# Hybrid trunk layer: attention as two head streams, residual on VectorE, gate weights side by side, and a planner that counts the overhead of a float32r product

## The chip, the cores and the metric

The kernel runs on one core of one Trainium2 chip. The metric is the time of one execution in microseconds (us) of device time, from the first to the last instruction with what the launch adds around them; lower is better. Engine names are those of the profile: PE is TensorE (matmuls), PEld its weight loads, DVE VectorE, ACT ScalarE, POOL GpSimd, SP the engine that only issues transfers.

## The reference

One layer of a trunk, for 1024 prompt tokens and 64 sample tokens (1088 columns in the kernel). One input projection feeds three token mixers and the gates; the three results are projected, gated, summed and projected once more.

```python
cols = x @ lw['w_in'] + lw['b_in']                       # 9864 columns
...
ya, ... = rwkv7_branch(a_cols, ...)                      # A: 8 heads x 64, a chain over chunks
yb, ... = mlstm_branch(b_qk, b_v, b_i, b_f, ...)         # B: 4 heads x 128; b_i, b_f have 4 columns each
yc = stick_breaking(heads_c(c_q), kc, vc, k_past, v_past)  # C: 8 heads x 64
ys = jnp.stack([ya * jax.nn.silu(a_z), yb * jax.nn.silu(b_z), yc * jax.nn.silu(c_z)], axis=2)
br = jnp.einsum('btnc,ncd->btnd', ys, lw['w_branch'])
g = jax.nn.sigmoid(gates.reshape(Bn, T, N_BRANCH, D_MODEL))
mix = jnp.sum(g * br, axis=2) @ lw['w_out']
x = layer_norm(DEEPNORM_ALPHA * x + mix, lw['ln_g'], lw['ln_b'])
x = x + (p @ lw['w_ple']) * jax.nn.sigmoid(x @ lw['w_ple_gate'])
```

Stick breaking, per head and block of 128 queries: z = q k / 8; A[t,s] is sigmoid(z_ts) times the product of 1 - sigmoid(z_tj) over s < j < t; the output is A v. The kernel makes the running product by a scan along the keys and A by the difference of neighbours.

## The kernel before, in words

**Products.** Large products are made in float32r. A number x is split into xh (its float32r rounding) and xl (the rest), a weight likewise into h and l, and a product is three matmuls, h·xh, h·xl and l·xh (`three`, L791). The input projection is 78 blocks of up to 128 columns; a block is 8 slices of the contraction times three token groups (`GR`: 384, 384 and 320 columns), so 72 matmuls. Splitting a block's weights is one ACT copy (h) and one DVE subtraction (l) (`wsplit`, L767). The block of the mLSTM gates has M = 36 columns: four input gates at 0 and four forget gates at 32.

**Order.** The kernel writes its own instruction order: it is one Python program that plans a clock for each engine while it emits. The main stream (`main`, L887) emits the blocks of the projection, then the merge of the three branches (`merge`, L1066), then the tail. Side tasks (generators) run beside it: an operation of a side task is emitted when the planned time at which its operands are ready has been reached by the planned clock of PE (`when`, `step`). So what `mm` (L313) counts for a float32r product (1 ns + columns / 2.4, or 213 ns below 256 columns) sets how many products of the main stream stand between two steps of a side task. DVE, ACT and POOL operations of side tasks are emitted when their engine's planned backlog is below 1.2 us. Among side tasks the lower priority number goes first (residual 3, the mixers' sequence 5).

**Sequence of the side tasks.** `side` (L980) runs the RWKV branch (A: fronts, inverses on POOL, chains over 17 chunks for each of four pairs of heads), then mLSTM (B), then attention (C), then `m_prep`, which takes memory and converts the first branch's result for the merge (`yconv(0)`, L1038: loads of `yd` and `yz` by SP, two DVE operations and one ACT copy for each of eight half tiles). The main stream begins the merge only when `m_prep` has set `prepared` (`m_begin`, L1031).

**The beginning.** An order written by hand (`INTRO`) normalises the input, transposes it and makes the first two blocks. Its last act is to spawn `resid` (L733), which scales and shifts the nine tiles of the normalised input in place by two POOL operations of 128x1024 each and stores them for the tail.

**Attention.** For each of four pairs of heads, `sbpair` (L1749) copies q and k of both heads into float32r parts, transposes v and then k (storing both), spawns for each head `sbhead` (scores, sigmoid, scan, difference) and `sbsum` (transposes of A and products with v), runs `sbsample` (the sample's attention over the cache), loads the next pair and waits until both heads' sums are done:

```python
for h in range(2):
    st = [0, 0]
    self.S.spawn(self.sbhead(p, h, R, st), f"C{p}{h}")
    self.S.spawn(self.sbsum(p, h, R, st, left), f"D{p}{h}")
yield from self.sbsample(p, R)
if p < 3:
    yield from self.sbload(p + 1, R)
yield lambda: left[0] == 0
```

The k transposes are kept in the buffer that is also head 1's scan buffer (`c1`); the v transposes in that of the sample.

Of the kernel before, what the change touches and what calls it, by code (L numbers as in the profile page):

```python
# [16 lines left out]
D = 1024  # L17
# [289 lines left out]
class K:  # L307
# [5 lines left out]
    def mm(self, out, lhsT, rhs, start, stop, more=False):  # L313
        n, w = fsize(out), 0.82 * fsize(lhsT)
        if lhsT.dtype == F32R:
            c = d = 1 + (213.0 if n < 256 else n / 2.4)
        else:
            d = 1 + 2 * n / 2.4
            c = d + max(d, w)
# [413 lines left out]
    def resid(self, xts):  # L733
# [8 lines left out]
        for t, x in enumerate(xts):  # L742
            m = 128 if t < 8 else 64
            for j, op in enumerate((OP.mult, OP.add)):
                yield self.tt(x[:m, :1024], x[:m, :1024], r3[:m, j, :], op, "g")
# [21 lines left out]
    def wsplit(self, i, e="v"):  # L767
# [5 lines left out]
        self.act(h[:, :kc, :M], r[:, :kc, :M], AF.Copy)  # L773
        self.tt(l[:, :kc, :M], r[:, :kc, :M], h[:, :kc, :M].bitcast(F32), OP.subtract, e)
# [16 lines left out]
    def three(self, b, i, g, k, hl, mh, ml):  # L791

        (kc, M), (h, l), (t0, n) = self.ws[i][1:], hl, GR[g]
        x1, x2 = mh[:, k, t0:t0 + n], ml[:, k, t0:t0 + n]
        self.mm(b[:M, :n], h[:, k, :M], x1, k == 0, False)
# [206 lines left out]
    def b_gates(self, i):  # L1002
# [719 lines left out]
    def c_all(self):  # L1722
# [26 lines left out]
    def sbpair(self, p, R):  # L1749
        self.S.note(f"   C {p}")  # L1750
        qs, O = R["qs"], self.O
        hp = slice(2 * p, 2 * p + 2)
        q, k, vv = R["q"], R["k"], R["svv"].r[:, :2304].rearrange("p (c h s d) -> p c h s d", h=2, s=2, d=64)
        for i in range(2):
            r, o = slice(64 * i, 64 * i + 64), slice(64 - 64 * i, 128 - 64 * i)
            x, y = R[f"sq{i}"], R[f"sk{i}"]
# [5 lines left out]
            yield self.tt(R[f"sl{i}"].r[r, :NT], k[r, :NT], y[r, :NT], OP.subtract)  # L1762
        for j, nm in ((2, "v"), (1, "k")):
            f, t = R[nm], R[nm + "t"]
            for c0 in (0, 4, 8):
                m = min(4, 9 - c0)
                w = 128 if c0 < 8 else 64
                b = yield from self.bank()
                for i in range(m):
                    o = (c0 + i) * 128  # L1770
                    yield self.tr(b[:w, i * 128:(i + 1) * 128], f[:, o:o + w])
                s = slice(c0 * 128, (c0 + m) * 128)
                yield self.act(t[:w, s], b[:w, :m * 128], AF.Copy)
                if nm == "v":
                    hi, lo = (vv[:w, c0:c0 + m, :, i, :] for i in range(2))
                    b4 = b[:w, :m * 128].rearrange("p (c h d) -> p c h d", h=2, d=64)
                    yield self.act(hi, b4, AF.Copy)
                    yield self.tt(lo, b4, hi.bitcast(F32), OP.subtract)
                self.unbank(b)
                yield  # L1780
            op, os = (O["sbk_p"], O["sbk_s"]) if j == 1 else (O["sbv_p"], O["sbv_s"])
            t3 = t.v(9, 128)
            yield self.dma(op[0, 0][:, hp, :].rearrange("(a t) h d -> t a (h d)", t=128), t3[:, 0:8, :], "s")
            yield self.dma(os[0, 0][:, hp, :].rearrange("t h d -> t (h d)"), t3[:64, 8, :], "s")
            if nm == "v":
                yield self.act(R["sv"][:64, :128], t[:64, 1024:1152], AF.Copy)
        left = [2]
        self.S.note(f"     heads {p}")
        for h in range(2):
            st = [0, 0]  # L1790
# [441 lines left out]
```

## Time and profile before

| | |
|---|---|
| time, median of 3 runs | 1767.66 us (1766.98 to 1769.55) |
| the profiled execution | 1766.9 us, of which span 1765.1 us |
| PE busy | 1711.2 us, 97% of the span |
| DVE, ACT, POOL busy | 1154.9 (65%), 792.6 (45%), 493.6 us (28%) |
| matmuls | 10873 |
| moved by DMA | 212.10 MB, mean 120 GB/s |
| mean granted TensorE clock | 0.994 |

How to read it: "busy" is the time in which at least one instruction of the engine runs. Matmuls are pipelined, so a busy PE can still be slower than its best; how many products pass in a stretch tells that. The granted clock is a share of 2.4 GHz: 1.00 is that level, 0.50 the level of 1.2 GHz. The kernel's stages in the span, by their instructions: the order by hand and the beginning of A up to about 200 us, A to about 704, B to about 968, C (attention) to about 1363, the merge to about 1534, then the tail.

### The profile page before, as it was taken

The numbers are of one execution on the slowest core, as the hardware profiler recorded it, in microseconds if no ns is written. First come the engines' busy times: TensorE is split into PE (matmuls) and PEld (weight loads), VectorE is DVE, ScalarE is ACT, GpSimd is POOL, SyncE is SP. The second block draws the span as 40 slices with busy tenths as digits, with TensorE's granted clock in tenths as the row PEclk, the third lists the DMA queues.
The fourth block names the chain that finished last, engine by engine and source line by source line (L and its number), as shares of the span: only waits on it lengthen the run. The fifth ranks groups of instructions, "written<-read, shape, count | busy, mean of one in ns | idle before, by whom it ended". The sixth has DMA issues, their size and how long they took to land.

```text
span 1765.1 us, 30061 instructions
## 1 busy us (share of the span) xinstructions
PE 1711.2 (97%) x10873; PEld 1587.3 (90%) x10873; DVE 1154.9 (65%) x2640; ACT 792.6 (45%) x1823; POOL 493.6 (28%) x969
## 2 busy tenths in 40 slices
PE   6979999999999999999999999999999899999999
PEld 5979987888888999999999999999999899988787
DVE  8476467686777655878643665757475568787743
ACT  6434455554445445454445555464553322322421
POOL 6644567266457341321011202111130000000100
PEclk9989999999999999999999999999999999999999
DMA  5533323323333333444335323343322877631421
GB/s 158 175 112 112 97 69 95 107 70 101 95 88 83 100 93 117 161 141 145 111 121 155 120 74 110 97 122 98 106 80 74 257 233 240 225 119 60 148 81 54
DMA packets 224635, 212.10 MB, mean 120 GB/s; under 512 B 53540, under 2 KB 192598, under 8 KB 224486
## 3 DMA queue, kind: packets, MB, share of 16 engines
q1 hardware_dynamic: 197518, 169.50, 32.3%
q10 hardware_dynamic: 22552, 29.02, 4.6%
q0 software_dynamic: 4416, 11.66, 2.1%
q8 instruction: 86, 1.41, 0.3%
q14 instruction: 63, 0.52, 0.1%
HBM read 136.81 MB, written 73.36 MB: 119 GB/s over the span
## 4 chain that ended last, share of the span: by engine, by line
PE 83%; DVE 9%; ACT 4%; issue 2%; DMA 1%; POOL 0%; ACTq 0%; SPq 0%; DVEq 0%; POOLq 0%
PE bk L321 78%; PE bk L328 5%; DVE heap L376 3%; ACT heap L353 3%; DVE heap L358 2%; DVE heap L371 2%; DVE whl L358 1%; DMA heap<-yz 1%; DMA heap<-in_x_prompt_dram 1%; ACT whl L353 0%; DVE heap L412 0%; DVE xl L358 0%; ACTq L431 0%; DVE heap L381 0%; DVE heap L409 0%
## 5 line engine op out<-in xcount | busy, mean ns | idle before, releaser
L321 PE MATMUL bk<-xh,whl 128*128 128x384 f32 (+3 forms) x3792 | 1057.5, 339 | 0.3 <-DVE heap L376 0.3
L321 PEld LDWEIGHTS bk<-xh,whl 128*128 128x128 f32 (+1 forms) x3792 | 682.1, 188 | 12.3 <-issue 3.4
L321 PE MATMUL bk<-xl,whl 128*128 128x384 f32 (+3 forms) x2184 | 669.6, 328 | 1.2 <-POOL xl L360 0.7
L321 PEld LDWEIGHTS bk<-xl,whl 128*128 128x128 f32 (+1 forms) x2184 | 404.4, 188 | 5.5 <-POOL xl L360 1.4
L353 ACT ACTIVATE heap<-bk 64x64 f32<-64x64 f32 (+9 forms) x679 | 219.5, 335 | 370.6 <-PE bk L321 147.8
L360 POOL TENSOR_TENSOR heap<-heap 32x30 f32<-32x30 f32 (+14 forms) x480 | 267.9, 558 | 36.3
L328 PE MATMUL bk<-ident,heap 128*128 128x128 f32 (+3 forms) x942 | 174.9, 277 | 14.1 <-ACT heap L353 12.1
L358 DVE TENSOR_TENSOR whl<-heap,whl 128x1024 fp32r<-128x1024 f32 (+1 forms) x114 | 122.8, 1079 | 91.0 <-ACT whl L353 84.8
L358 DVE TENSOR_TENSOR heap<-heap 128x256 f32<-128x256 f32 (+16 forms) x352 | 168.0, 483 | 11.8 <-DMA heap<-yz 3.4
L321 PE MATMUL bk<-heap 128*128 128x128 f32 (+7 forms) x886 | 157.6, 293 | 8.7 <-ACT heap L353 7.8
L353 ACT ACTIVATE heap<-bk,pc 128x384 f32<-128x384 f32 (+5 forms) x218 | 114.1, 548 | 104.5 <-PE bk L321 79.8
L328 PEld LDWEIGHTS bk<-ident,heap 128*128 128x128 f32 (+3 forms) x942 | 119.7, 142 | 29.6 <-issue 14.9
L321 PEld LDWEIGHTS bk<-heap 128*128 128x128 f32 (+3 forms) x886 | 117.8, 182 | 30.7 <-ACT heap L353 19.9
L353 ACT ACTIVATE whl<-heap 128x1024 fp32r<-128x1024 f32 (+1 forms) x116 | 105.3, 911 | 72.8 <-PE bk L321 54.7
L353 ACT ACTIVATE heap<-heap 64x64 f32<-64x64 f32 (+10 forms) x330 | 113.1, 347 | 45.4 <-DVE heap L376 18.4
L321 PE MATMUL bk<-heap,heap 32*32 32x32 f32 (+3 forms) x1058 | 125.7, 244 | 6.9 <-ACT heap L353 6.4
L321 PEld LDWEIGHTS bk<-heap,heap 128*128 128x128 f32 (+2 forms) x1058 | 98.7, 152 | 31.7 <-ACT heap L353 17.6
L401 DVE TENSOR_TENSOR_SCAN heap<-heap,cst 128x512 f32<-128x512 f32 (+8 forms) x68 | 96.2, 1417 | 45.6 <-POOL heap L418 26.1
L321 PE MATMUL bk<-heapr,whl 128*128 128x384 f32 (+2 forms) x648 | 118.0, 341 | 4.6 <-ACT heapr L353 4.0
L321 PE MATMUL bk<-heapr 128*128 128x256 f32 (+2 forms) x524 | 119.4, 329 | 0.0
L321 PEld LDWEIGHTS bk<-heapr,whl 128*128 128x128 f32 x648 | 110.0, 191 | 10.4 <-ACT heapr L353 5.1
L353 ACT ACTIVATE heap<-bk,hb 128x384 f32<-128x384 f32 (+1 forms) x120 | 67.6, 563 | 113.0 <-PE bk L321 94.7
(154 smaller groups left out, 1819.6 us busy)
## 6 DMA issues: line engine op xcount, KB each, us to landing
heap<-in_w_in_dram SPq DMA_DIRECT2D x77, 512.0 KB
heap<-gt SPq DMA_DIRECT2D x24, 544.0 KB
gt<-heap ACTq DMA_DIRECT2D x48, 192.0 KB
heap<-crd SPq DMA_DIRECT2D x12, 544.0 KB
heap<-yd SPq DMA_DIRECT2D x24, 272.0 KB
heap<-yz SPq DMA_DIRECT2D x24, 272.0 KB
heap<-in_w_branch_dram SPq DMA_DIRECT2D x24, 256.0 KB
xsd<-heap SPq DMA_DIRECT2D x24, 192.0 KB
```

The lines of the kernel that those rows point to most:

```text
L321: lambda: self.nc.tensor.matmul(out, lhsT, rhs, start=start, stop=stop, skip_group_check=more),
L328: lambda: self.nc.tensor.transpose(out, in_, self.ident[:p, :p]), load=(0.82 * fsize(in_), d))
L353: return self.nc.scalar.activation(out, in_, func, **kw)
L358: lambda: self.nc.vector.tensor_tensor(out=out, in0=a, in1=b, op=op))
L360: lambda: self.nc.gpsimd.tensor_tensor(out=out, in0=a, in1=b, op=op))
L371: lambda: q.tensor_scalar(out=out, in0=a, scalar1=s1, scalar2=s2, op0=op0, **kw))
L376: lambda: self.nc.vector.scalar_tensor_tensor(out=out, in0=a, scalar=s, in1=b, op0=op0, op1=op1))
L401: return self.S.emit("dve", fsize(out) * 2.13 + 90, rd, [out], lambda: self.nc.vector.tensor_tensor_scan(out=out, data0=d0, data1=d1, init ...
```

## The change

Four edits. (1) The planner counts 13 ns instead of 1 ns over the columns of a float32r product. (2) The residual's two operations per tile go from POOL (128x1024) to DVE (two halves of 128x512 each). (3) The gate block's l is written into columns 64 to 99 of h, so that one matmul of 100 columns makes h·x and l·x; two matmuls (for xh and xl) take the place of three, and DVE adds the two halves of the result before the store, which the ACT queue issues. (4) Attention is three kinds of tasks: one sequence that loads a pair, transposes k and v and runs the sample, and one stream for each head, which goes to the next pair's copies and scores when its own sums of the last pair are done. Head 1 also waits for the k transposes; the values' transposes wait for both heads' sums of the last pair; the sums wait for the values.

```diff
     def mm(self, out, lhsT, rhs, start, stop, more=False):
         n, w = fsize(out), 0.82 * fsize(lhsT)
         if lhsT.dtype == F32R:
-            c = d = 1 + (213.0 if n < 256 else n / 2.4)
+            c = d = 13 + (213.0 if n < 256 else n / 2.4)
...
             for j, op in enumerate((OP.mult, OP.add)):
-                yield self.tt(x[:m, :1024], x[:m, :1024], r3[:m, j, :], op, "g")
+                for o in (0, 512):
+                    yield self.tt(x[:m, o:o + 512], x[:m, o:o + 512], r3[:m, j, o:o + 512], op)
             yield self.dma(self.resd[t, :m], x[:m, :1024], "s")
...
         self.act(h[:, :kc, :M], r[:, :kc, :M], AF.Copy)
+        if M < 64:
+            l = h[:, :, 64:]
         self.tt(l[:, :kc, :M], r[:, :kc, :M], h[:, :kc, :M].bitcast(F32), OP.subtract, e)
...
+        if M < 64:
+
+            for j, x in enumerate((x1, x2)):
+                self.mm(b[:64 + M, :n], h[:, k, :64 + M], x, k + j == 0, k == kc - 1 and j == 1)
+            return
         self.mm(b[:M, :n], h[:, k, :M], x1, k == 0, False)
         self.mm(b[:M, :n], h[:, k, :M], x2, False, False)
         self.mm(b[:M, :n], l[:, k, :M], x1, False, k == kc - 1)
...
                 self.act(d[r, :n], bank[r, :n], AF.Identity, bias=self.gb[r, 0:1])
+                self.tt(d[r, :n], bank[64 + 32 * j:68 + 32 * j, :n], d[r, :n], OP.add)
                 self.dma(gd[j, :, t0:t0 + n], d[r, :n], "a")
...
-        yield from self.sbload(0, B)
+        self.cld = self.ckt = self.cvt = 0
+        self.cpr, self.csm = [0, 0], [0, 0]
+        for h in range(2):
+            self.S.spawn(self.sbheads(h, B), f"C{h}")
         for p in range(4):
             yield from self.sbpair(p, B)
+        yield lambda: min(self.csm) == 4
...
     def sbpair(self, p, R):
...
+        yield from self.sbload(p, R)
+        self.cld = p + 1
+        yield lambda: min(self.cpr) > p
+        yield from self.sbturn(p, R, 1, "k")
+        self.ckt = p + 1
+        yield lambda: min(self.csm) >= p
+        yield from self.sbturn(p, R, 2, "v")
+        self.cvt = p + 1
+        self.S.note(f"     values {p}")
+        yield from self.sbsample(p, R)
+
+    def sbheads(self, h, R):
+
+        r, o = slice(64 * h, 64 * h + 64), slice(64 - 64 * h, 128 - 64 * h)
+        q, k, x, y, qs = R["q"], R["k"], R[f"sq{h}"], R[f"sk{h}"], R["qs"]
+        for p in range(4):
+            yield lambda: self.cld > p
             yield self.act(x.r[r, :NT], q[r, :NT], AF.Copy)
             yield self.tt(x.r[o, :NT], q[r, :NT], x[r, :NT], OP.subtract)
...
+            self.cpr[h] = p + 1
+            yield lambda: self.csm[h] >= p and (h == 0 or self.ckt > p)
+            self.S.note(f"     head {p}{h}")
+            st = [0, 0]
+            self.S.spawn(self.sbsum(p, h, R, st), f"D{p}{h}")
+            yield from self.sbhead(p, h, R, st)
...
+    def sbturn(self, p, R, j, nm):
...
-        yield lambda: left[0] == 0
...
-    def sbsum(self, p, h, R, st, left):
+    def sbsum(self, p, h, R, st):
...
+        yield lambda: self.cvt > p
         for G in range(4):
...
-        left[0] -= 1
+        self.csm[h] = p + 1
```

`sbturn` holds the transposes, copies and stores that stood in `sbpair`, for one of k and v; the order of the two is turned round.

## Rows read from the trace of the kernel before

**Rows 1.** The page, part 1: busy time, share of the span and number of instructions of each engine.

```profile
PE 1711.2 (97%) x10873; PEld 1587.3 (90%) x10873; DVE 1154.9 (65%) x2640; ACT 792.6 (45%) x1823; POOL 493.6 (28%) x969
```

**Rows 2.** Busy time by stretch, two stretches of the merge; columns: stretch in us from the span's start, its length, busy us of each engine with the number of its instructions in brackets, granted clock of PE, share of the DMA engines, GB/s.

```profile
1408.00:1452.00 44.00, 44.00 (x268) 44.00 (x267) 29.36 (x52) 9.78 (x16) 0.00 (x0) 1.00 0.73 232
1452.00:1496.00 44.00, 44.00 (x270) 44.00 (x269) 36.52 (x69) 10.21 (x18) 1.16 (x2) 1.00 0.76 246
```

**Rows 3.** Groups of PE instructions, each shape apart, whole run: the products of the gate block. Columns: line, engine, operation, names, contraction*weight columns, partitions x columns, count, busy us, mean ns of one.

```profile
L321 PE MATMUL bk<-xh,whl 128*36 128x384 f32 x32 | 8.8, 341 | 0.0
...
L321 PE MATMUL bk<-xl,whl 128*36 128x384 f32 x16 | 5.4, 336 | 0.0
...
L321 PE MATMUL bk<-xh,whl 128*36 128x320 f32 x16 | 4.8, 339 | 0.0
...
L321 PE MATMUL bk<-xl,whl 128*36 128x320 f32 x8 | 2.5, 308 | 0.0
```

**Rows 4.** What PE waited for, stretch 60 to 112 us. Columns: us in total, times, longest us.

```profile
PE bk L321 <- DVE heap L376: 11.8, 1, 11.8
```

**Rows 5.** POOL in order of time, 60 to 105 us: start, us, line, operation, count; L360 with 128x1024 is the residual.

```profile
60.09 4.93 POOL L360 TENSOR_TENSOR heap<-heap,heap 128x1024 f32<-128x1024 f32 x2 [6.31 <-ACT heap L353]
...
78.43 13.41 POOL L360 TENSOR_TENSOR heap<-heap,heap 128x1024 f32<-128x1024 f32 x5
...
92.11 12.60 POOL L360 TENSOR_TENSOR heap<-heap,heap 128x1024 f32<-128x1024 f32 x5
```

**Rows 6.** Groups of DVE instructions, shapes apart, 84.87 to 109 us (columns as in rows 3; idle time before them at the end).

```profile
L358 DVE TENSOR_TENSOR heap<-heap 128x256 f32<-128x256 f32 x4 | 5.8, 1474 | 0.0
L371 DVE TENSOR_SCALAR heap<-heap,der 128x256 f32<-128x256 f32 x2 | 4.7, 2342 | 0.0
L401 DVE TENSOR_TENSOR_SCAN heap<-cmask,heap 128x256 f32<-128x256 f32 x1 | 2.8, 2773 | 0.0
...
L376 DVE SCALAR_TENSOR_TENSOR heap<-bk,der,heap 128x384 f32<-128x384 f32 x2 | 1.2, 606 | 0.0
```

**Rows 7.** The same view, 116 to 135 us, where POOL runs nothing but copies of one column.

```profile
L358 DVE TENSOR_TENSOR heap<-heap 128x256 f32<-128x256 f32 x4 | 1.6, 418 | 0.0
L376 DVE SCALAR_TENSOR_TENSOR heap<-bk,der,heap 128x384 f32<-128x384 f32 x2 | 1.2, 618 | 3.0 <-ACT heap L353 1.7 <-issue 1.3
...
L371 DVE TENSOR_SCALAR heap<-heap,der 128x256 f32<-128x256 f32 x2 | 0.7, 367 | 0.0
...
L401 DVE TENSOR_TENSOR_SCAN heap<-cmask,heap 128x256 f32<-128x256 f32 x1 | 0.7, 692 | 0.0
```

**Rows 8.** Busy time by stretch around that wait (columns as in rows 2).

```profile
60.00:84.87 24.87, 24.87 (x152) 24.29 (x151) 8.41 (x13) 9.16 (x20) 24.47 (x14) 1.00 0.62 206
...
97.47:109.46 11.99, 0.17 (x1) 0.00 (x0) 11.95 (x11) 0.00 (x0) 10.89 (x6) 0.67 0.20 78
...
109.46:115.16 5.70, 5.70 (x20) 5.52 (x20) 2.01 (x6) 1.20 (x4) 0.00 (x0) 0.50 0.19 66
```

**Rows 9.** DVE groups of the whole run: the nearest forms to the new operations.

```profile
L358 DVE TENSOR_TENSOR heap<-heap 128x512 f32<-128x512 f32 x23 | 15.8, 688 | 0.5
...
L358 DVE TENSOR_TENSOR heap<-bk,heap 64x256 f32<-64x256 f32 x32 | 13.2, 413 | 23.1 <-ACT heap L353 22.9
```

**Rows 10.** The chain that ended last, 1362 to 1400 us: start, us, what.

```profile
1374.07 3.71 DMA heap<-yz
...
1386.37 3.21 DMA heap<-yz
...
1391.97 8.09 PE bk L321 x39
```

**Rows 11.** Busy time by stretch: the first products of the merge (columns as in rows 2).

```profile
1380.87:1395.00 14.13, 9.53 (x35) 7.00 (x34) 6.88 (x10) 3.67 (x6) 0.00 (x0) 0.76 0.82 264
```

**Rows 12.** The queue of SP in order of time: the first load of the conversion for the merge.

```profile
1363.64 0.53 SPq L431 DMA_DIRECT2D heap<-yd  x1
```

**Rows 13.** DVE in order of time, from the last scan of one pair of heads to the first of the next.

```profile
1035.57 2.30 DVE L401 TENSOR_TENSOR_SCAN heap<-heap,cst 128x1024 f32<-128x1024 f32 x1 [1.48 <-POOL heap L423]
...
1054.54 0.42 DVE L358 TENSOR_TENSOR heap<-bk,heap 64x256 f32<-64x256 f32 x1 [2.33 <-ACT heap L353]
...
1073.16 0.42 DVE L401 TENSOR_TENSOR_SCAN heap<-heap,cst 128x128 f32<-128x128 f32 x1 [4.75 <-POOL heap L418]
```

**Rows 14.** Busy time by stretch: A, B and C (columns as in rows 2).

```profile
200.00:704.00 504.00, 487.68 (x3508) 438.19 (x3507) 342.22 (x1138) 254.36 (x757) 250.05 (x470) 1.00 0.34 94
704.00:968.00 264.00, 263.46 (x1718) 255.87 (x1717) 169.96 (x451) 127.95 (x296) 53.61 (x128) 1.00 0.44 139
968.00:1364.00 396.00, 395.97 (x2604) 383.17 (x2603) 253.50 (x291) 209.61 (x384) 69.48 (x207) 1.00 0.33 98
```

**Rows 15.** What PE waited for, stretch 200 to 704 us (columns as in rows 4).

```profile
PE bk L321 <- ACT heap L353: 14.2, 27, 1.6
```

**Rows 16.** Groups of PE instructions, the main stream's products of 384 columns (columns as in rows 3): first two 200 to 704 us, last two 968 to 1364 us.

```profile
L321 PE MATMUL bk<-xh,whl 128*128 128x384 f32 x795 | 245.0, 355 | 0.0
L321 PE MATMUL bk<-xl,whl 128*128 128x384 f32 x397 | 133.3, 336 | 0.0
...
L321 PE MATMUL bk<-xh,whl 128*128 128x384 f32 x699 | 206.1, 345 | 0.0
L321 PE MATMUL bk<-xl,whl 128*128 128x384 f32 x349 | 117.2, 336 | 0.0
```

More of the change, by code (lines that the diff above doesn't have):

```diff
@@ L1750, in sbpair @@
         self.S.note(f"   C {p}")
[L1751 to L1756, printed above, removed]
+        yield from self.sbload(p, R)
[13 more added lines that the diff above has]
+            yield lambda: self.cld > p
             yield self.act(x.r[r, :NT], q[r, :NT], AF.Copy)
@@ L1761, in sbpair @@
             yield self.act(y.r[o, :NT], k[r, :NT], AF.Copy)
[L1762 to L1784, printed above, removed]
-            if nm == "v":
-                yield self.act(R["sv"][:64, :128], t[:64, 1024:1152], AF.Copy)
@@ L1787, in sbpair @@
[L1787 to L1790, printed above, removed]
-            self.S.spawn(self.sbhead(p, h, R, st), f"C{p}{h}")
-            self.S.spawn(self.sbsum(p, h, R, st, left), f"D{p}{h}")
-        yield from self.sbsample(p, R)
-        if p < 3:
-            yield from self.sbload(p + 1, R)
-        yield lambda: left[0] == 0
+            yield self.tt(R[f"sl{h}"].r[r, :NT], k[r, :NT], y[r, :NT], OP.subtract)
+            self.cpr[h] = p + 1
@@ new lines, in sbheads @@
+            yield lambda: self.csm[h] >= p and (h == 0 or self.ckt > p)
[4 more added lines that the diff above has]
+    def sbturn(self, p, R, j, nm):
+        O = self.O
+        hp = slice(2 * p, 2 * p + 2)
+        vv = R["svv"].r[:, :2304].rearrange("p (c h s d) -> p c h s d", h=2, s=2, d=64)
+        f, t = R[nm], R[nm + "t"]
+        for c0 in (0, 4, 8):
+            m = min(4, 9 - c0)
+            w = 128 if c0 < 8 else 64
+            b = yield from self.bank()
+            for i in range(m):
+                o = (c0 + i) * 128
+                yield self.tr(b[:w, i * 128:(i + 1) * 128], f[:, o:o + w])
+            s = slice(c0 * 128, (c0 + m) * 128)
+            yield self.act(t[:w, s], b[:w, :m * 128], AF.Copy)
+            if nm == "v":
+                hi, lo = (vv[:w, c0:c0 + m, :, i, :] for i in range(2))
+                b4 = b[:w, :m * 128].rearrange("p (c h d) -> p c h d", h=2, d=64)
+                yield self.act(hi, b4, AF.Copy)
+                yield self.tt(lo, b4, hi.bitcast(F32), OP.subtract)
+            self.unbank(b)
+            yield
+        op, os = (O["sbk_p"], O["sbk_s"]) if j == 1 else (O["sbv_p"], O["sbv_s"])
+        t3 = t.v(9, 128)
+        yield self.dma(op[0, 0][:, hp, :].rearrange("(a t) h d -> t a (h d)", t=128), t3[:, 0:8, :], "s")
+        yield self.dma(os[0, 0][:, hp, :].rearrange("t h d -> t (h d)"), t3[:64, 8, :], "s")
+        if nm == "v":
+            yield self.act(R["sv"][:64, :128], t[:64, 1024:1152], AF.Copy)
```

## The prediction

> **What bounds the kernel now.** I read the busy times first. PE is busy for 97% of the span, no other engine for more than 65% [rows 1]. So a gain must take work off PE or close a hole in it. Next I looked at what PE can do at best. In two stretches of the merge, 88 us with no side work, 538 products pass, 163.6 ns each [rows 2]. Their columns go 384, 384, 320 (`GR`), on average 362.7, which stream in 151.1 ns at 2.4 GHz. The rest, 12.5 ns, is the overhead that the first edit counts. Then I read the stretches by stage: B and C have almost no hole, 0.5 us in 264 and 0.03 us in 396, and A has 16.3 us in 504 [rows 14]. Two more holes stand out, one before A, one where the merge begins [rows 4, 11]. The kernel is therefore PE's work plus a few holes, and side work costs time only where PE waits for it.
>
> **The change part by part.**
>
> *Gate block.* Now 32 + 16 + 16 + 8 = 72 products [rows 3]; afterwards 48. The 24 that go have the usual mix of widths, so 24 x 163.6 ns = 3.9 us [rows 2]. The block lies in a stage where PE has nearly always something to do, so I take all of it: **-3.9 us**. Added are six DVE additions of 4x384; the nearest form, 64x256 from PSUM, takes 0.41 us [rows 9], so six are some 3 us on an engine with room. The store of each is issued by ACT, which now waits for DVE six times. Behind it in ACT's queue stand the activations of the first front and chain of A, and PE waits for those. The planner counts this wait, so the order moves rather than PE stopping: 0 to 2 us, and I take 0.
>
> *Residual.* PE stands still for 11.8 us before a product of A's first front, waiting for DVE [rows 4]. The DVE list of that stretch says why. A 256-column operation with both inputs in SBUF takes 1474 ns, a tensor_scalar 2342, a scan 2773 [rows 6]. The same forms take 418, 367 and 692 ns in the stretch from 116 us on [rows 7]. An operation that reads PSUM takes 606 against 618, no difference [rows 6, 7]. What differs is POOL: in the first stretch it runs the residual, 2.5 us each, back to back [rows 5]. The four plus two plus one operations of these rows alone cost 5.8 + 4.7 + 2.8 = 13.3 us instead of 1.6 + 0.7 + 0.7 = 3.0 us, 10.3 us of the hole. The planner knows nothing of this, so it put PE's product too early. With the residual on DVE, POOL is empty here, and the slowing goes. When PE comes back it runs for 5.70 us at a granted clock of 0.50, that is at 1.2 GHz after 11.8 us of standing still [rows 4, 8]; at 2.4 GHz this work takes half, so 2.8 us more go. Sum: **-14.6 us**.
>
> What DVE pays: 9 tiles x 2 operations x 2 halves = 36 of 128x512, 688 ns each [rows 9], 24.8 us. They can start at about 61 us, when POOL now starts [rows 5]. From 60 to 84.87 DVE is busy for 8.4 of 24.9 us [rows 8], so some 16.5 us fit there, six tiles of 2.75 us. Three tiles, 8.3 us, meet the front. The front's hole would then come back only as far as the planner misjudges DVE, and DVE's planned price (1.04 ns a column + 68, 600 ns) is 88 ns short of the row, 1.1 us over twelve operations. Bounds for what is left of the hole: 0 to 8.3 us. I take 0, since the planner counts DVE's queue.
>
> The Trainium skill (SBUF — State Buffer, section Who interferes with whom) says that a DVE instruction with two SBUF inputs and a GpSimd instruction that reads SBUF exclude each other, and the second to issue waits for the whole of the first. By that rule seven front operations would each wait for up to one POOL operation of about 2.5 us, 17 us, more than the 10.3 us that the rows give; in both cases the hole goes, and the sum by the rule is the same. The rule also says that the residual's DVE operations, which have two SBUF inputs, could themselves block POOL; POOL has only one-column copies there.
>
> *Attention and the start of the merge.* The merge begins at 1380.87, and its first 35 products take 14.13 us instead of 35 x 163.6 ns = 5.7 us [rows 11]: a hole of 8.4 us, part standing still, part a lower granted clock (0.76 on average). The chain there runs over loads of `yz` up to 1391.97 [rows 10]. They belong to `yconv(0)`, which starts at 1363.64, when attention's last sum is stored [rows 12], and takes 28.3 us. It has to start 11.1 us earlier against the main stream for the hole to go.
>
> Two parts of the change bring it forward. First the streams: from the end of one pair's last sum (1054.96) to the next pair's first scan (1073.16) pass 18.2 us [rows 13] of copies and transposes, beside which no scan runs. There are three such boundaries. Afterwards a head's copies run under its own last sums, and only scores, sigmoid and select stand between. If I take half, 9 us each, attention ends 27 us earlier; 3.7 us each would do. New waits: head 1 stands behind the k transposes, which need both heads' copies, and the sums stand behind the values' transposes. They delay a head's first query blocks, the short ones. Second the count: 12 ns more for each product means fewer products of the main stream between two steps of a side task. A has about 1192 x 1.5 = 1790 main products, C 1048 x 1.5 = 1570 [rows 16]; 12 ns each are 21 and 19 us that the side gains on the main stream at most. Either alone is enough, so the hole goes: **-8.4 us**. An attention that ends still earlier gains nothing more, since PE has no hole in C [rows 14].
>
> *The count.* It is also the part that can cost. The 12 ns not counted were cover: a side task's product stood behind more main products than planned. In A PE waits for ACT 27 times, 14.2 us [rows 15], where the slowing of DVE by POOL's inverses makes chains late. Each such wait grows by 12 ns times the products in front, five or six, about 65 ns: 27 x 65 ns = 1.8 us. Bounds: if every gap in A were without slack, +21 us; if the new order happens to miss these waits, -14 us. I take **+2 us**, by the waits that are there. In B and C, where PE waits for 0.5 us in 660 us [rows 14], I take 0.
>
> **Sum.** -3.9 - 14.6 - 8.4 + 2 = -24.9 us against the profiled execution's 1766.9 us (span 1765.1 and 1.8 around it): 1742.0. The median of the runs lies 0.8 us above that execution, so I say 1743.
>
> **The rivals.**
>
> *Slower: the lost cover.* Place: A, B and C, wherever a side product is put earlier than its operand is really there. Price: at most 12 ns for each main product, 21 us in A, 19 in C, and in B, by its length against A's, some 15; 55 us in all, which would give 1743 - 2 + 55 = 1796. It decides from about 30 us on, that is when over half of the gaps have no slack. Against it: B and C show hardly a wait, so their gaps are not near the edge [rows 14]. The Trainium skill (TensorE: Matmul & The Clock Gate, section Back-to-back issue gap) would feed this rival: it gives 2.5 ns over columns / 2.4 for a warm product, by which 13 counts 10 ns too many. The trace here has 12.5 ns, so the measurement decides.
>
> *DVE takes POOL's place.* The front's operations queue behind the residual, and up to 8.3 us of the hole stay: 1743 + 8 = 1751.
>
> *Attention does not end earlier*, because DVE (253.5 of 396 us busy in C [rows 14]) or the new waits hold the streams: the hole of 8.4 us stays, 1751.
>
> *A gets worse by chance of order*, its 16 us of holes becoming 25: 1752. Or it gets better, or fewer changes between side and main products cost PE less: about 1735.
>
> *Only the products count*, nothing else moves: 1767.7 - 3.9 = 1764.
>
> **How the numbers follow.** The forecast with small variations of A has 0.57; DVE in POOL's place 0.09; attention's hole stays 0.08; A worse 0.09; better 0.10; only the products 0.04; slower 0.03. Leaving out the last two and the ends of the others gives 1732 to 1755 for 8 in 10. 0.2% is 3.5 us, about what a measurement of this kernel can tell from no change. Only "slower" lies above it, 0.03; of "only the products" most lies within it: 0.03; faster has 0.94.
>
> **What would show each step.** Gate block: 48 products with 100 weight columns. Residual: no DVE operation of 256 columns above 1 us between 80 and 110 us, no long wait of PE there, granted clock 1.00. Merge: the first load of `yd` long before the main stream's last block ends, and 35 products in about 5.7 us. Boundaries in C: the next pair's first scan a few us after the last sum instead of 18. Count: PE's waits in A at 14 to 20 us, still none in B and C. The prediction is wrong if PE waits in B, C or the tail for whole microseconds, or if the residual's DVE work opens a new hole before 110 us.

## The result: slower, where a gain of 25 us was forecast

The changed kernel takes 1779.07 us (median; 1776.5 to 1782.1) against 1767.32 us of the kernel before in the same job: ratio 1.0066, 95% interval 1.0047 to 1.0085. The forecast was 1743 us, 1732 to 1755. The profiled execution took 1782.09 us, of which the span is 1780.4.

First the page's busy times of the changed kernel, then its busy time by stretch (columns as in rows 2).

```profile
PE 1717.7 (96%) x10849; PEld 1592.0 (89%) x10849; DVE 1161.3 (65%) x2682; ACT 791.8 (44%) x1823; POOL 451.7 (25%) x951
...
0.00:200.00 200.00, 181.95 (x1109) 173.00 (x1110) 138.96 (x310) 97.16 (x205) 72.98 (x141) 0.99 0.47 142
88.00:132.00 44.00, 44.00 (x282) 43.15 (x280) 27.11 (x64) 18.70 (x45) 2.74 (x6) 1.00 0.37 109
200.00:704.00 504.00, 469.84 (x3344) 422.76 (x3343) 341.42 (x1124) 247.41 (x745) 247.09 (x465) 0.98 0.32 89
704.00:924.00 220.00, 214.95 (x1387) 205.57 (x1386) 147.45 (x420) 99.03 (x243) 44.86 (x119) 0.99 0.41 129
1320.00:1452.00 132.00, 132.00 (x805) 132.00 (x804) 38.98 (x60) 30.77 (x49) 1.25 (x6) 1.00 0.48 153
```

The kernel before, the stretches that were not shown:

```profile
0.00:200.00 200.00, 171.74 (x1033) 163.59 (x1034) 127.17 (x246) 90.83 (x190) 113.95 (x152) 0.97 0.43 130
704.00:924.00 220.00, 219.46 (x1443) 212.05 (x1442) 154.65 (x432) 104.72 (x259) 44.52 (x110) 1.00 0.43 138
```

Both holes that the prediction wanted closed are closed: 88 to 132 us and 1320 to 1452 us, with the merge's first product at 1404 in it, are full at a granted clock of 1.00 (before 0.76 at the merge's start [rows 11], and 11.8 us of waiting in front of A [rows 4]). The loss lies between. Count PE's instructions: 76 more by 200 us than before, then 164 fewer in A (before 3508 [rows 14]) and 56 fewer from 704 to 924. At 924 us the changed kernel is 144 behind. Of these it need not do 24, the gate block's. 120 x 163.6 ns [rows 2] = 19.6 us late; the merge's start gives back 8.4; 11.2 remain. The medians differ by 11.75 us. The profiled executions, in which the counting is done, differ by 15.2 (1782.09 against 1766.9), so some 4 us of theirs arise behind 924 us.

What PE waited for in A, 200 to 704 us (columns as in rows 4):

```profile
PE bk L321 <- ACT heap L353: 23.3, 38, 3.3
PE bk L321 <- DVE heap L376: 5.0, 3, 2.6
PE bk L328 <- DVE heap L358: 3.8, 4, 2.1
PE bk L328 <- DVE heap L376: 0.4, 1, 0.4
```

That is 32.5 us in 46 waits, where before had 15.7 in 31. On top of it there are five stretches in A at a granted clock of 0.50, 17.1 us together, of which up to half is lost; before, A had none. Four of the five stand right behind A's four longest waits (3.28, 2.58, 2.09 and 1.71 us), the fifth, at 266.5 us, begins in a run of 34 products of 32x32, behind no wait above 0.32 us. The one behind the longest wait is shown further down; the others (columns as in rows 2):

```profile
266.50:269.90 3.40, 3.40 (x27) 3.34 (x26) 2.79 (x6) 2.65 (x12) 3.16 (x4) 0.50 0.02 5
474.70:478.10 3.40, 3.40 (x11) 3.28 (x12) 2.76 (x6) 0.22 (x1) 3.19 (x3) 0.50 0.04 10
491.70:495.10 3.40, 3.40 (x15) 3.40 (x16) 2.06 (x7) 0.83 (x4) 2.93 (x7) 0.51 0.00 0
549.80:553.20 3.40, 3.40 (x12) 3.40 (x11) 2.51 (x6) 1.29 (x5) 3.09 (x5) 0.50 0.00 0
```

One wait in full. PE, DVE and POOL in order of time around 413 us (start, us, line, operation, count), then the stretches of the wait and behind it:

```profile
412.97 0.34 PE L321 MATMUL bk<-xh,whl 128*128 128x384 f32 x1
416.58 0.76 PE L321 MATMUL bk<-heap 128*128 128x128 f32 x2 [3.28 <-ACT heap L353]
...
411.60 0.84 DVE L376 SCALAR_TENSOR_TENSOR heap<-heap,pc,heap 128x256 f32<-128x256 f32 x1
412.36 0.81 DVE L358 TENSOR_TENSOR heap<-heap,heap 128x256 f32<-128x256 f32 x1
413.10 0.70 DVE L371 TENSOR_SCALAR heap<-heap 128x128 f32<-128x128 f32 x1
413.72 0.97 DVE L376 SCALAR_TENSOR_TENSOR heap<-heap,pc 128x128 f32<-128x128 f32 x2
414.61 0.72 DVE L376 SCALAR_TENSOR_TENSOR heap<-heap,pc,heap 128x64 f32<-128x64 f32 x1
415.26 0.21 DVE L358 TENSOR_TENSOR heap<-heap,heap 128x64 f32<-128x64 f32 x1
415.50 0.52 DVE L376 SCALAR_TENSOR_TENSOR heap<-heap,pc 128x64 f32<-128x64 f32 x1
416.06 0.23 DVE L381 COPY heap<-bk 64x64 f32<-64x64 f32 x1
...
409.14 8.18 POOL L360 TENSOR_TENSOR heap<-heap 32x210 f32<-32x210 f32 x11
...
412.97:416.58 3.61, 0.34 (x2) 0.02 (x1) 3.25 (x8) 0.22 (x1) 3.30 (x5) 1.00 0.00 0
416.58:419.50 2.92, 2.92 (x10) 2.52 (x11) 1.27 (x3) 1.33 (x5) 2.60 (x5) 0.51 0.00 0
```

PE's product at 416.58 needs ACT's copy, ACT needs DVE's copy of 64x64, and that stands in DVE's queue behind eight operations, seven of them of another task (A's front, `a_front`; the copy is the chain's, `a_chain`). From 411.60 to 416.06 these take 4.46 us. By the formulas in `tt`, `ts` and `stt` the planner counts them at 396 + 334 + 197 + 2 x 263 + 197 + 135 + 197 = 1982 ns. So the plan is 2.5 us short, and PE stands still for 3.28 us. POOL's inverse runs beside all the while. Behind the wait the clock is at half.

Where the shortfall comes from: DVE groups of the changed kernel, first row 398 to 436 us, where POOL works on an inverse, the other three 436.5 to 457.5 us, where it works on none.

```profile
L371 DVE TENSOR_SCALAR heap<-heap 128x128 f32<-128x128 f32 x4 | 2.0, 496 | 0.1
...
L358 DVE TENSOR_TENSOR heap<-heap 128x256 f32<-128x256 f32 x3 | 1.3, 418 | 0.1
L371 DVE TENSOR_SCALAR heap<-heap 128x128 f32<-128x128 f32 x4 | 1.1, 282 | 0.1
L381 DVE COPY heap<-bk 64x64 f32<-64x64 f32 x4 | 0.9, 217 | 0.7 <-PE bk L321 0.6
```

The planner has 334, 197 and 135 ns for the last three: 82 to 85 ns short with POOL out of the way, and 299 ns short for the tensor_scalar beside an inverse. (That POOL is the reason for this second part is read from such rows; no run took the inverses away.) The Trainium skill (VectorE: DVE Perf Modes, section The TRN2 errata) gives an fp32 tensor_tensor add (columns + 151) / 0.96 ns, measured at 512 and 2048 columns; the estimate by that page for 256 columns is 424 ns. The row's 418 agrees with it. The planner's 1.04 ns a column fits as well; its fixed 68 ns is what falls short.

### The profile page after: what moved, and what is told of

Same layout as the page of the kernel before. It is cut to its first block, busy times and chain, and to the rows that moved or that the text cites. A ratio compares the mean times of both kernels' runs of the same rounds, so it can differ in the third digit from the quotient of the medians.

```text
span 1780.4 us, 30008 instructions
## 1 busy us (share of the span) xinstructions
PE 1717.7 (96%) x10849; PEld 1592.0 (89%) x10849; DVE 1161.3 (65%) x2682; ACT 791.8 (44%) x1823; POOL 451.7 (25%) x951
## 4 chain that ended last, share of the span: by engine, by line
PE 49%; issue 3%; DVE 1%; DMA 1%; ACT 1%; POOL 1%; SPq 0%; ACTq 0%; POOLq 0%; DVEq 0%
PE bk L321 46%; PE bk L328 3%; DMA heap<-yz 1%; DVE heap L376 0%; ACT heap L353 0%; DMA heap<-in_w_branch_dram 0%; DVE heap L358 0%; ACT heapr L353 0%; POOL heap L418 0%; DVE heapr L376 0%; POOL heap L382 0%; ACT whl L353 0%; DVE whl L358 0%; POOL hb L371 0%; SPq L431 0%
## 5 line engine op out<-in xcount | busy, mean ns | idle before, releaser
L321 PE MATMUL bk<-xh,whl 128*128 128x384 f32 (+1 forms) x3768 | 1056.7, 341 | 0.8 <-DVE xh L381 0.5
L321 PEld LDWEIGHTS bk<-xh,whl 128*128 128x128 f32 x3768 | 684.8, 190 | 10.6 <-issue 3.8
L353 ACT ACTIVATE heap<-bk 64x64 f32<-64x64 f32 (+10 forms) x679 | 218.4, 335 | 367.0 <-PE bk L321 139.2
L360 POOL TENSOR_TENSOR heap<-heap 32x30 f32<-32x30 f32 (+14 forms) x480 | 264.4, 551 | 36.4
L358 DVE TENSOR_TENSOR heap<-heap 128x256 f32<-128x256 f32 (+17 forms) x364 | 172.4, 480 | 13.9 <-DMA heap<-yz 5.5
L321 PE MATMUL bk<-heap 128*128 128x128 f32 (+7 forms) x928 | 161.0, 288 | 18.3 <-ACT heap L353 15.5
L321 PE MATMUL bk<-heap,heap 128*128 128x128 f32 (+3 forms) x1016 | 129.4, 252 | 10.7 <-ACT heap L353 8.4
L401 DVE TENSOR_TENSOR_SCAN heap<-heap,cst 128x128 f32<-128x128 f32 (+8 forms) x68 | 96.6, 1421 | 37.3 <-POOL heap L423 19.8
L376 DVE SCALAR_TENSOR_TENSOR heap<-heap 128x4 f32<-128x4 f32 (+9 forms) x263 | 87.1, 333 | 50.5 <-ACT heap L353 45.0
L321 PE MATMUL bk<-heapr,whl 128*128 128x384 f32 (+2 forms) x648 | 114.0, 335 | 0.5 <-DVE heap L376 0.5
```

The costliest lines, as they stand in the source:

```text
L321: lambda: self.nc.tensor.matmul(out, lhsT, rhs, start=start, stop=stop, skip_group_check=more),
L353: return self.nc.scalar.activation(out, in_, func, **kw)
L358: lambda: self.nc.vector.tensor_tensor(out=out, in0=a, in1=b, op=op))
L360: lambda: self.nc.gpsimd.tensor_tensor(out=out, in0=a, in1=b, op=op))
L376: lambda: self.nc.vector.scalar_tensor_tensor(out=out, in0=a, scalar=s, in1=b, op0=op0, op1=op1))
L401: return self.S.emit("dve", fsize(out) * 2.13 + 90, rd, [out], lambda: self.nc.vector.tensor_tensor_scan(out=out, data0=d0, data1=d1, init ...
```

## The experiments

**The parts alone.** *e1: the whole change but the count.*

```diff
-            c = d = 13 + (213.0 if n < 256 else n / 2.4)
+            c = d = 1 + (213.0 if n < 256 else n / 2.4)
```

> The changed kernel with only the count undone: a float32r product counts 1 ns over its columns again. Theory 'lost cover' (the 12 ns more put side products too early, so PE waits in A and B and falls to 1.2 GHz after the waits): the holes of A and B go back to about those of the kernel before (some 16 us of standing still in A, no stretch at 0.50 after 116 us), the holes at 97 us and at the merge stay away: 1740 to 1750 us. Theory 'shifted order' (the residual on DVE and the earlier front move A against POOL's inverses, and the count is not the cause): 1770 to 1780 us, with A's waits still above 28 us.

Measured: 1747.53 us, ratio to before 0.9881 (0.9866 to 0.9896). Busy time by stretch:

```profile
0.00:200.00 200.00, 183.50 (x1124) 174.79 (x1125) 137.27 (x303) 97.49 (x206) 71.02 (x135) 1.00 0.47 141
200.00:704.00 504.00, 481.22 (x3497) 438.98 (x3496) 342.86 (x1131) 254.29 (x754) 250.59 (x471) 1.00 0.34 94
704.00:924.00 220.00, 217.77 (x1411) 210.81 (x1410) 147.13 (x413) 101.35 (x247) 43.85 (x105) 0.99 0.42 130
```

By 924 us it has done 15 + 153 + 24 = 192 products more than the changed kernel: 192 x 163.6 ns = 31.4 us. The medians differ by 31.5 us, the profiled executions by 35.7, so 4.3 of theirs arise behind 924 us. So the count costs 31.5 us, most of it before 924 us, and without it the change is 20 us faster than before: it is the whole reason why the change is slower. What PE waited for in A, 200 to 704 us:

```profile
PE bk L321 <- ACT heap L353: 16.4, 34, 1.6
PE bk L321 <- DVE heap L376: 4.8, 7, 1.7
PE bk L328 <- DVE heap L386: 0.4, 1, 0.4
```

*e2: the kernel before with nothing but the count* (1 to 13 in the same line).

> The kernel before with only the count changed to 13 ns. 'Lost cover': the side tasks end earlier, so the merge's hole of 8.4 us goes, the hole of 11.8 us at 97 us stays, and A and B lose some 35 to 45 us: 1785 to 1805 us. 'Shifted order': only the merge's hole goes, 1757 to 1762 us.

1789.37 us, ratio 1.0116 (1.0101 to 1.0131). Waits in A 30.2 us, 20.5 us at 0.50 there, and the hole at the merge's start is gone, as forecast: attention's last scan starts at 1303 instead of 1343 us. The count has the effect without the other edits too.

*e3: the kernel before with nothing but the residual on DVE.*

```diff
-                yield self.tt(x[:m, :1024], x[:m, :1024], r3[:m, j, :], op, "g")
+                for o in (0, 512):
+                    yield self.tt(x[:m, o:o + 512], x[:m, o:o + 512], r3[:m, j, o:o + 512], op)
```

> The kernel before with only the residual on DVE. 'Lost cover': the hole at 97 us and the stretch at 1.2 GHz behind it go, 14.6 us, A's waits stay within a few us of 16, the side tasks start A some 10 us earlier and the merge's hole of 8.4 us shrinks: 1745 to 1755 us. 'Shifted order': the earlier front lands A's chains on POOL's inverses, A's waits grow by 15 us or more: 1765 to 1780 us.

1773.38 us, ratio 1.0029 (1.0019 to 1.0038): slightly slower, though the hole in front of A is gone and 91 products more are done by 200 us. A gives back 43 of them (waits 23.0 us for 15.7, 13.7 us at 0.50 for none), and the merge's start, no longer covered, grows from 4.5 to 10.2 us of waits and from 6.8 to 23.9 us at 0.50. A gain ahead of a stage shifts that stage's main stream against its side chains, and the chains did not come earlier with it: attention's last scan starts at 1349. The time is that expected for "shifted order", but A's waits grew by 7.3 us and not by 15.

*e4: the kernel before with nothing but the head streams* (`sbheads`, `sbturn` and the rest of the attention hunks).

```diff
+        for h in range(2):
+            self.S.spawn(self.sbheads(h, B), f"C{h}")
...
-        yield lambda: left[0] == 0
```

> The kernel before with only attention as two head streams. Both theories: A and B are untouched, attention ends some 27 us earlier or more, and the merge's hole of 8.4 us goes: 1757 to 1762 us. If the streams bring nothing, 1767 us and the hole is still there.

1758.17 us, ratio 0.9944 (0.9929 to 0.9958): -9.2 us for -8.4 forecast. A is as before (15.0 us of waits).

*f4: residual and streams, count 1, gate block as before* (the hunks of e3 and e4 together).

> The kernel before with the residual on VectorE and the two head streams, count 1, and the gate weights as before (three products to a step). It tells what the gate edit is worth, and what the residual is worth once the head streams are there. If the terms add up: the gate edit 3.9 us, so 1751.4 us, and the residual the rest, 6.8 us below the 1758.2 us of the streams alone. If the residual's whole 14.6 us come out once the hole at the start of the merge is gone, 1743.6 us, and then the gate edit costs 4 us rather than saving any. If each edit mostly changes the order of the second stage, anything from 1745 to 1775 us.

1753.22 us, ratio 0.9915 (0.99 to 0.9929). The residual is worth 5.0 us beside the streams, not 14.6, and the gate edit 5.7 (1753.22 - 1747.53), not 3.9. Neither is clean: f4's profiled execution has 13.7 us at 0.50 in A and e1's none, up to half of which, 6.9 us, is time, so the order of A may move as much as the edits do.

**How the loss depends on the count.** *f1: the changed kernel, count 7 in the place of 13.*

> The changed kernel with a float32r product counted as its columns plus 7 ns, between the 1 ns that gave 1747.5 us and the 13 ns that gave 1779.1 us. Theory 'lost cover' (each nanosecond more in the count lets the scheduler put side products that much earlier, and the cover that the too short count gave is used up little by little): half of the difference or less, 1752 to 1766 us, with waits of TensorE between 200 and 704 us between the 21.6 us of count 1 and the 32.5 us of count 13, and two to five stretches at a granted clock of 0.50 rather than one or seven. Rival 'chance of order' (any count makes another order, and 13 happened to make a bad one): no relation to the count, as likely below 1750 or above 1775 as between.

1757.14 us, ratio 0.9937 (0.9923 to 0.9952), waits in A 24.3 us: 1, 7 and 13 give 1747.5, 1757.1 and 1779.1. The time rises with the count, which speaks against an accident of one order. In the profiled executions the time at 0.50 in A is 17.1 us at 7 as at 13, so the 22 us between these two are not the clock's.

*g3: 13 until A's chains are done, 1 from there on.*

```diff
+            c = d = (13 if self.afdone >= 0 and self.acdone < 4 else 1) + (213.0 if n < 256 else n / 2.4)
```

> The changed kernel with count 13 until the chains of the second stage are done, and 1 from there on. If the loss is made in the second stage alone (where GpSimd's inverses run beside and VectorE's small operations take longer than the scheduler counts): 1770 to 1780 us, as the whole change. If the count does harm wherever it stands, and the second stage is only the longest: 1758 to 1770 us.

1774.59 us, ratio 1.0031 (1.0018 to 1.0044); waits in A 31.9 us. 27 of the 31.5 us are lost up to the end of A's chains.

**Giving the cover back.** *f2: count 13, and a side task's product is held back by 200 ns.*

```diff
-SLACK = {"pe": 0.0, "act": 250.0, "dve": 250.0, "pool": 250.0, "dma": 0.0}
+SLACK = {"pe": -200.0, "act": 250.0, "dve": 250.0, "pool": 250.0, "dma": 0.0}
```

> The changed kernel with count 13, but a product of a side task is put into the order only when its inputs were due 200 ns earlier by the scheduler's own clock (the margin for pe goes from 0 to -200 ns). Theory 'lost cover': the margin gives back what the longer count took away, so the waits of TensorE between 200 and 704 us fall from 32.5 us to 15 to 24 us, the stretches at granted clock 0.50 go from seven to at most two, and the time is 1742 to 1757 us. Rival 'the longer count does harm by another way' (other work of the stages moved against the main products, transfers asked for at other times): margin or not, 1768 to 1790 us.

1856.01 us, ratio 1.0502 (1.0481 to 1.0524): a miss, and in part a badly built one. `when` subtracts the margin from every dependence, that on PE's own last product into the same bank included, so groups of small products were drawn apart. The waits in A do fall, to 20.7 us, as expected; but attention's last scan starts at 1429 and the merge's start has 35.7 us of waits.

*g1: the margin where it was meant, in `dep`, and only for what a product takes from another engine or a transfer.*

```diff
-                t = max(t, float((w + np.where(m[1][p, f] == e, OWN[e], LAT[m[1][p, f]])).max()))
+                t = max(t, float((w + np.where(m[1][p, f] == e, OWN[e], LAT[m[1][p, f]] + (250.0 if e == 0 else 0.0))).max()))
```

> The changed kernel, count 13, with the margin set where f2 set it wrongly: f2's 200 ns also counted between two products into the same bank, so that groups of small products were pulled apart. Here a product is due 250 ns later only after what another engine or a transfer wrote for it. Theory 'lost cover' (250 ns is about what 12 ns for each of some 20 products between two steps of a chain took away): waits of TensorE between 200 and 704 us 12 to 24 us instead of 32.5, at most three stretches at granted clock 0.50 in that window, 1740 to 1758 us. Rival 'side chains pay for any delay': fewer waits, but the chains of the second stage and of attention end later, the hole at the start of the merge comes back, 1768 to 1860 us.

1755.19 us, ratio 0.9942 (0.9921 to 0.9962). 23.9 of the 31.5 us come back with the count left at 13. The waits fell less than expected (27.2 us, 12 to 24 expected), the time at 0.50 more, from 17.1 to 6.8 us. That time changes between executions of one kernel: g1's five go from 1753.2 us at a mean granted clock of 1.000 to 1762.6 at 0.994, and the profiled one, 1761.2, is one of the long ones.

*g4: count 13, and 100 ns more for each DVE operation of the four commonest kinds until A's chains are done* (`over` is 168 there, 68 elsewhere; the same in `ts`, `stt` and `cp`).

```diff
-            return self.S.emit("dve", fsize(out) * 1.04 + 68, [a, b], [out],
+            return self.S.emit("dve", fsize(out) * 1.04 + self.over, [a, b], [out],
```

> The changed kernel, count 13, with 100 ns more counted for each operation of VectorE until the chains of the second stage are done (in this stretch its small operations took 85 to 240 ns more than counted). Theory 'two short counts held each other': the short count of a product had covered the short count of VectorE's work, so counting both truly gives back most of the loss: 1740 to 1760 us, waits between 200 and 704 us 14 to 25 us. Rival 'only products matter': no better than 1770 us.

1746.27 us, ratio 0.988 (0.9864 to 0.9897). The whole loss is gone with the count at 13. What PE waited for in A:

```profile
PE bk L321 <- ACT heap L353: 14.6, 28, 2.5
PE bk L321 <- DVE heap L382: 1.2, 3, 0.7
PE bk L321 <- DVE heap L364: 0.5, 1, 0.5
```

16.3 us, and no time at 0.50. By [rows 2] the count of 13 is the true price of a product where no side work runs. What made it a loss is that the 1 had given cover. That much g1 and g4 show together; that the cover was needed because DVE's price is 82 to 299 ns an operation too low is read from the rows above, since g1 gives back most of the loss without touching DVE's price.

**Too much cover.** *f3: count 1 and f2's margin with 100 ns.* (`SLACK["pe"]` is -100.)

> The changed kernel with count 1 and a margin of 100 ns for the side tasks' products. Theory 'lost cover', carried on: the 21.6 us of waits that count 1 leaves between 200 and 704 us are of the same kind, and fall to 12 to 18 us; 1735 to 1745 us against 1747.5 us. Rival 'the cover that count 1 gives is enough, what is left are chains that set their own pace': no change beyond the spread of orders, 1744 to 1756 us.

*g2: count 1 and g1's edit with 120 ns.*

> Count 1 with 120 ns more before a product that follows another engine. Theory 'lost cover': the 21.6 us of waits between 200 and 704 us fall below 16 us and the time is 1735 to 1746 us. Rival 'side chains pay for any delay': 1748 to 1830 us, with waits at the start of the merge.

*h1: count 1 and g4's 100 ns for DVE.*

> The changed kernel with count 1 and 100 ns more for each VectorE operation until the second stage's chains are done; beside the run that has count 13 and the same 100 ns (1746.3 us). If the count matters only because VectorE's work was counted too short, the two are within 5 us of each other: 1741 to 1751 us. If the count of 13 is a loss of its own that the 100 ns outweigh, 1725 to 1740 us. If cover beyond what is needed delays the side chains, as in the run with count 1 and 120 ns before products: 1748 to 1770 us, with waits at the start of the merge.

*h2: g4, and 100 ns more for ACT's operations too.*

```diff
-        c = fsize(out) * 0.833 + 93 * (len(rd) - 1) + (51 if psum(in_) else 93)
+        c = fsize(out) * 0.833 + 93 * (len(rd) - 1) + (51 if psum(in_) else 93) + self.over - 68
```

> Count 13 and 100 ns more for VectorE's and also ScalarE's operations in the same stretch. If the waits that are left there (16.3 us between 200 and 704 us, 14.6 of them on ScalarE) come from ScalarE's short count: waits below 12 us and 1735 to 1745 us. If the chains then come late, as with a margin on every product: fewer waits, but 1748 to 1790 us and waits of TensorE at the start of the merge.

f3 1829.71 us (ratio 1.0347, 1.031 to 1.0384), g2 1750.99 (0.9903, 0.9888 to 0.9918), h1 1779.39 (1.0064, 1.0047 to 1.0081), h2 1756.78 (0.9937, 0.9922 to 0.9952). Each has fewer waits in A than the kernel it is made from, h2 only 3.9 us, and none is faster. f3 and h1 lie beyond every range that was expected for them. 1741 to 1751 us was expected of h1 if the count matters only through DVE's short price, and it took 1779.4: by these runs it counts how much cover there is in all, not which price is true. In each the merge's start has lost what A won; in h1, 1310 to 1545 us:

```profile
PE bk L321 <- ACT heapr L353: 18.8, 14, 7.1
PE bk L321 <- DVE heapr L364: 7.8, 5, 2.8
```

All runs together. The time is the median of at least four executions; the other columns are from one, the profiled. "At 0.50" is time at that granted clock. The kernel before took 1767.1 to 1768.4 us beside each group of runs.

| kernel | time, us | A: waits, us (times) | A: at 0.50, us | attention's last scan, us | merge's start: waits, us | at 0.50, us |
|---|---|---|---|---|---|---|
| before | 1767.3 | 15.7 (31) | 0 | 1343 | 4.5 | 6.8 |
| after | 1779.1 | 32.5 (46) | 17.1 | 1274 | 0.5 | 0 |
| e1 | 1747.5 | 21.6 (42) | 0 | 1314 | 0 | 0 |
| e2 | 1789.4 | 30.2 (41) | 20.5 | 1303 | 0 | 0 |
| e3 | 1773.4 | 23.0 (38) | 13.7 | 1349 | 10.2 | 23.9 |
| e4 | 1758.2 | 15.0 (29) | 0 | 1300 | 0.7 | 0 |
| f4 | 1753.2 | 22.2 (35) | 13.7 | 1303 | 0 | 0 |
| f1 | 1757.1 | 24.3 (45) | 17.1 | 1284 | 0 | 0 |
| g3 | 1774.6 | 31.9 (45) | 20.5 | 1285 | 0 | 0 |
| g1 | 1755.2 | 27.2 (40) | 6.8 | 1263 | 0 | 0 |
| g4 | 1746.3 | 16.3 (32) | 0 | 1306 | 0 | 0 |
| g2 | 1751.0 | 18.5 (30) | 3.4 | 1326 | 7.3 | 13.7 |
| h2 | 1756.8 | 3.9 (9) | 13.7 | 1338 | 15.5 | 27.3 |
| h1 | 1779.4 | 8.1 (19) | 13.7 | 1365 | 28.5 | 47.7 |
| f3 | 1829.7 | 14.8 (23) | 37.5 | 1411 | 25.7 | 44.4 |
| f2 | 1856.0 | 20.7 (27) | 13.7 | 1429 | 35.7 | 64.8 |

The two ends of the table are two ways to lose. Little cover: side products come early, PE waits in A, and the clock falls. Much cover: every step of a side chain stands behind more main products, the chains take longer (h1's last 128-row bn_stats of A, a late step of its chains, starts at 792 us, e1's at 713), and from a last scan at 1326 us on PE waits where the merge begins. Up to 1314 these waits are 0.7 us at most. Where PE waits, the merge's first product comes 23 to 37 us behind the last scan (h2 23, before 37); where it does not, 55 us and more. e1 and g4 lie between; their intervals overlap, and both beat the two kernels of this case by about 20 and 32 us. The rest of the count's effect, an attention that ends at 1274 instead of 1314, bought nothing, since 1314 is early enough. Before itself, at 1343, was a little late for its merge and had the cover that A needs.

## Why the prediction was wrong, step by step

**What held.** PE is the bound, and products done by a given time price the whole: two differences, 11.2 and 31.4 us, come out of counts, to within some 4 us of those of the profiled executions. *The hole in front of A* went, and for the reason given: DVE from 80 to 110 us of the changed kernel,

```profile
L358 DVE TENSOR_TENSOR heap<-heap,heap 128x512 f32<-128x512 f32 x11 | 7.2, 684 | 0.0
L358 DVE TENSOR_TENSOR heap<-heap 128x256 f32<-128x256 f32 x6 | 2.5, 415 | 0.0
L371 DVE TENSOR_SCALAR heap<-heap,der 128x256 f32<-128x256 f32 x4 | 1.5, 372 | 0.0
L401 DVE TENSOR_TENSOR_SCAN heap<-cmask,heap 128x256 f32<-128x256 f32 x2 | 1.4, 680 | 0.0
```

with 415, 372 and 680 ns where POOL's residual had made it 1474, 2342 and 2773 [rows 6]; the new operations take 684 ns, as taken from [rows 9]. *The merge's start*: full, and e4 alone gave 9.2 us for 8.4. *The pair boundary* closed further than the half that was taken: from 37.6 us between the last scan of one pair and the first of the next [rows 13] to 14.7, and that first scan starts 6.6 us before the pair's last sum (the 64x256 operation) instead of 18.2 us behind its end,

```profile
1013.60 2.30 DVE L401 TENSOR_TENSOR_SCAN heap<-heap,cst 128x1024 f32<-128x1024 f32 x1 [2.46 <-POOL heap L423]
1028.33 0.42 DVE L401 TENSOR_TENSOR_SCAN heap<-heap,cst 128x128 f32<-128x128 f32 x1 [0.80 <-POOL heap L418]
...
1034.97 0.42 DVE L358 TENSOR_TENSOR heap<-bk,heap 64x256 f32<-64x256 f32 x1
```

and by e4 the last scan comes 43 us earlier than before, 27 forecast. *The gate block* has its 48 products with 100 weight columns,

```profile
L321 PE MATMUL bk<-xh,whl 128*100 128x384 f32 x16 | 5.7, 356 | 0.0
L321 PE MATMUL bk<-xl,whl 128*100 128x384 f32 x16 | 5.3, 334 | 0.0
L321 PE MATMUL bk<-xh,whl 128*100 128x320 f32 x8 | 2.4, 318 | 0.0
L321 PE MATMUL bk<-xl,whl 128*100 128x320 f32 x8 | 2.4, 308 | 0.0
```

(16 + 16 + 8 + 8 for the 72 of [rows 3]), but its own gain could not be read apart from A's order: 5.7 us between f4 and e1, 3.9 forecast.

**The step that failed** is "The count", +2 us; it is +31.5. Four things in it were wrong.
1. *The size of one wait's growth.* Five or six products in front of a late step were assumed, 65 ns. A late step stands behind a whole run of DVE work: in the wait shown 4.46 us, the time of some 27 products. From e1 to after a wait of A grew from 0.51 us (21.6 / 42) to 0.71 (32.5 / 46), by three times the 65 ns; 10.9 us in all.
2. *The clock.* The estimate had no term for it. Five stretches at 0.50 in A, 17.1 us, cost at most half of that, 8.6 us. It can be less: e1's execution at a mean granted clock of 0.999 took 1746.4 us, two at 0.996 took 1748.1 and 1748.3, so some 5 us of lost clock went with 1.8 us of time. In [rows 14] A stands at 1.00 although it has 16 us of holes; that a few longer waits would bring the clock down could not be read there.
3. *The stages taken at 0.* From 704 to 924 us 24 products fewer than e1, 3.9 us; before 200 us 15 fewer, 2.5 us. PE waits for 4.8 us from 704 to 924 us (e1 2.1, before 0.5), the sign of being wrong that the prediction named. A stage without a wait is not a stage with slack.
4. *The lead that was in hand.* The prediction worked out that a 512-column operation of DVE is planned 88 ns too short, and used it for twelve operations of the residual. The same fixed 68 ns stand in most of A's 1124 DVE operations. The short count of a product was the other half of that error: g4 shows that counting both costs nothing.

10.9 + 8.6 + 3.9 + 2.5 = 25.9 of the 31.4 us; the other 5.5, or more where the clock cost less, lie in A, and no view names them.

The rival "slower: the lost cover" had the place and the mechanism, at most 21 us in A and 55 in all. Its bound for A did not hold: A lost 153 products, 25.0 us, since a wait's growth and the clock are not limited to 12 ns for each product. (Its 15 us for B should be 11 by the lengths that it names, 264 against 504 us; nothing hangs on that.) Its chance of 0.03 came from "B and C show hardly a wait", but A was nearly enough alone, and the point from which it decides, some 30 us, was just reached. The Trainium skill's 2.5 ns over columns / 2.4 (TensorE: Matmul & The Clock Gate, section Back-to-back issue gap), which the page gives for an isolated matmul and not for a stream of them, pointed the right way for a reason that the trace does not bear out. By [rows 2] 13 is the price, and the loss came with the cover that the 1 had given.

**The second step that was too large** is the residual's -14.6: it is +6.0 alone (e3) and -5.0 beside the streams (f4 against e4). The front gained, 91 products by 200 us, 14.9 us. What failed is the silent assumption that a gain ahead of A goes through A unchanged. Alone, A gives back 43 products, 7.0 us, and the merge's start some 14 (5.7 us more waits and half of 17.1 us more at 0.50). Why A's waits rose in e3, from 31 to 38, was not tried by a run of its own. It may be the main stream's place against POOL's inverses or against the chains.

## What to carry to other kernels

A list scheduler's prices are right only against each other: before one of them is made truer, check the prices on the other engines in the same stage, and correct them together. Cover has an optimum: too little is paid in waits and in the matmul clock, too much in chains that end after the main stream needs them, so look at both places, the waits in the stage and the deadline behind it. A gain in front of a stage is not yet a gain; read how many products are done behind the stage.

## What the runs showed of the hardware that I had not expected

TensorE's granted clock can fall while PE never waits. In h2 PE has no wait at all from 400 to 440 us. Busy time by stretch there, and in the first line for an earlier stretch of h2:

```profile
297.70:300.90 3.20, 3.20 (x45) 2.17 (x45) 1.25 (x5) 0.01 (x1) 2.72 (x7) 1.00 0.00 0
...
419.00:422.50 3.50, 3.50 (x21) 3.25 (x19) 2.14 (x7) 1.85 (x3) 0.00 (x0) 1.00 0.02 5
422.50:425.30 2.80, 2.80 (x43) 1.95 (x43) 1.52 (x11) 0.40 (x1) 0.00 (x0) 1.00 0.22 76
425.30:438.50 13.20, 13.20 (x66) 9.88 (x67) 4.06 (x18) 2.90 (x15) 0.00 (x0) 0.51 0.02 6
```

From 422.5 to 425.3 us PE ran 36 products of 32x32 with six single 128-column transposes between them, after a full run of main products. Then the clock is at 0.50, that is 1.2 GHz, and stays there for 13 us with PE busy throughout. So it is in h1, where 13.7 us at 0.50 begin at 229.4 us behind 32 such products, without a wait since 215 us; and the changed kernel's stretch at 266.5 us begins among such products. That they are the reason is not shown: at 297.7 us h2 ran 36 of them too, with five main products and four others between, without a wait, and the clock stayed at 1.00; and the kernel before ran 15 groups of 20 or more of them in A, its clock at 1.00 throughout. What tells the cases apart no run shows. An instruction order with few waits, as in h2 and h1, can still have 13.7 us at 0.50 in A.
